# A hybrid attention layer on one core: the products with the values' weights take high and low parts at once, and VectorE's order is changed in three places

## The chip, the core and the metric

The kernel runs on one core of a Trainium2 chip. The metric is device time in microseconds. A core has five engines with queues of their own: TensorE (PE, with its weight loads as PEld), VectorE (DVE), ScalarE (ACT), GpSimd (POOL) and SyncE (SP, which here only issues DMAs). SBUF is the working memory of 128 partitions, PSUM the memory into which TensorE writes. In the profile's rows a name like L510 is line 510 of the kernel before.

## What is computed

One layer: an adaptive layer norm whose scale and shift come from a conditioning vector, a combined input projection, two groups of eight attention heads (forgetting attention with a softmax, and stick-breaking attention), SiLU gates, an output projection and a residual layer norm. Sequence 1024, width 1024, head width 64, all in float32.

```python
mod = jax.nn.silu(c) @ w_ada[layer] + b_ada[layer]       # shift, scale, gate
u = _layer_norm(x) * (1.0 + scale[:, None, :]) + shift[:, None, :]
h = u @ w_in[layer]
...
# forgetting heads, block of 128 queries
s = einsum(q, k) * scale + (f_q[..., :, None] - f_k[..., None, :])
p = softmax(where(causal, s, -inf));  out = einsum(p, v)
...
# stick-breaking heads
w = where(strict, exp(log_beta + later), 0.0);  out = einsum(w, v)
...
y = concatenate([y_fox, y_sb]) @ w_out[layer]
x = _layer_norm(alpha * x + gate[:, None, :] * y, ln_g, ln_b)
```

## The kernel before

**Two parts for each number.** Every operand of a large product is held as a rounded high part (float32r) and the remainder, the low part. A product is then high times high, low times high and high times low, added in PSUM. The high parts are made by ScalarE or GpSimd, the remainders by VectorE or GpSimd.

**The start (lines 141 to 718).** x, the conditioning weights (`wss`, one tile of 2 x 1024 columns for each of eight blocks of the width, in three buffers) and the first weights come by SP's queue in a fixed order. `mod_part` (L228) is one VectorE pass over 1024 columns that gives one block's scale or shift, so two passes a block. `u_turn` (L240) transposes x on TensorE into the PSUM tile `xT_early`; `u_round` (L246, L247) makes u's high part and the full u on ScalarE, in that same tile; `u_rest` (L259) makes the remainder on VectorE, after which the tile is free for the next block's transposes. In the loop over `kb` TensorE runs eight products of block kb's high part, transposes block kb+1, and then runs the products with the remainder. `in_turn` chains VectorE's passes in the order in which the code calls them: for kb above 1 both modulation passes of block kb+2 first, and then the remainder of block kb+1.

**The attention (lines 425 to 545 and 1031 to 1063).** Eight pairs of heads, p = 0 to 3 stick-breaking and 4 to 7 forgetting; a unit is (pair, head, block i of 128 queries), 128 in all. In iteration k of the main loop TensorE runs the scores of unit k into the one tile S (`att_scores`, L455, L456), a piece of other work from `fillers` (projections of later pairs, marked m and v), then the value products that are ready (`att_pv`, L522), then the transposes of unit k-2 (`att_transpose`, L507), and fillers again. The transposes go by groups of up to four key blocks into one of two tiles T; ScalarE copies the group's high part (L509) and VectorE subtracts for the low part (L510), into two tiles of `pt`, one for the high and one for the low parts. These remainders are the list `lows`. A unit with i of 4 or more has two groups.

**The value product.** When both units of a block j of 256 queries are transposed, `att_pv` multiplies the 2j+2 key blocks with the values, first all high parts and then all low parts, into 256 columns of PSUM. The weights are the 128 columns [v high, v low] of a head, so half of the partitions hold the product with v's high part and the others that with its low part; ScalarE copies one half (L529), VectorE adds it to the other (L530), GpSimd multiplies by the gate (L531).

**Scores.** For a forgetting head VectorE adds the forget terms to S and takes the maximum in one pass (L462), and ScalarE's exponential, a reciprocal and GpSimd's scaling follow. For a stick-breaking head ScalarE makes two sigmoids of S (L476, L478), VectorE a scan (L483, L487), GpSimd a product (L489).

**What sets the order.** TensorE's order is that of the code throughout, SP's too up to the end of the start. On the other engines a scheduler orders the work by a timeline that it models, and `after(...)` holds an instruction behind given ones. `HELD` names the iterations in which halves of the first pair's q and k, kept in SBUF as `st_held`, are written out (L269 for q, L282 for k).

Of the kernel before, what the change touches and what calls it, by code (L numbers as in the profile page):

```python
# [13 lines left out]
P = 128  # L14
# [13 lines left out]
def tile_hybrid_layer(  # L28
# [29 lines left out]

    def pt_tile(which, name, dt=F32R, shape=None):
        return big("pth" if which == 0 else "ptl", 3, name, dt, shape)  # L60

# [12 lines left out]
    RING = 5  # L74
    WARM = (4, 1, 1, 1, 0)
    NORM_ON = {6: nc.vector, 7: nc.vector}
# [65 lines left out]
    c_sb = cp.tile([P, NB], F32, tag="c_sb", name="c_sb")  # L142
    xt, wss_sb = [], []
# [299 lines left out]
    def att_scores(u, following):  # L443
# [14 lines left out]
        if p >= 4:  # L458
            a = att_tile(f"a_{p}_{h}_{i}")
            nm = sb.tile([P, 1], F32, tag="nm", bufs=4, name=f"nm_{p}_{h}_{i}")  # L460
            l = sb.tile([P, 1], F32, tag="l", bufs=4, name=f"l_{p}_{h}_{i}")
            nc.vector.tensor_tensor_reduce(out=v3(a), in0=S[:, :ns, :w], in1=v3(f),  # L462
                                           op0=ALU.add, op1=ALU.min, scale=-1.0, scalar=BIG,
                                           accum_out=nm)
            if following:
# [27 lines left out]

    def att_transpose(u):
        p, h, i = u
        a = st_w.pop(u)
        j, qo = i // 2, (i % 2) * P
        for g in range((i // 4) + 1):
            n = min(4, i + 1 - 4 * g)
            if (p, h, j, g) not in st_pt:  # L500
                st_pt[p, h, j, g] = [pt_tile(x, f"pt{x}_{p}_{h}_{j}_{g}", F32R, [P, 4, 256])
                                     for x in range(2)]
            hi, lo = st_pt[p, h, j, g]
            tp = t_tile(f"T_{p}_{h}_{i}_{g}")
            for b in range(n):
                kb = 4 * g + b
                nc.tensor.transpose(tp[:, b * P:(b + 1) * P], a[:, kb * P:(kb + 1) * P], ident)  # L507
            t3 = tp[:, :n * P].rearrange("p (a b) -> p a b", a=n)
            nc.scalar.copy(hi[:, :n, qo:qo + P], t3)  # L509
            lows[:] = [nc.vector.tensor_tensor(lo[:, :n, qo:qo + P], t3, hi.bitcast(F32)[:, :n, qo:qo + P],  # L510
                                               op=ALU.subtract)]

    y_last = []

    def att_pv(p, h, j):
        acc = pv_tile(f"pv_{p}_{h}_{j}")
        last = 2 * j + 1
        for part in range(2):
            for kb in range(last + 1):
                pt = st_pt[p, h, j, kb // 4][part]  # L520
                q0 = P if kb == last else 0
                nc.tensor.matmul(acc[:, q0:256], vt[p][:, kb, h * P:(h + 1) * P], pt[:, kb % 4, q0:],  # L522
                                 start=(part == 0 and kb == 0), stop=(part == 1 and kb == last))
        r = slice(h * HD, h * HD + HD)
# [4 lines left out]
        nc.scalar.copy(tm[r, :], acc[o, :256])  # L529
        nc.vector.tensor_tensor(yt[r, :], acc[r, :256], tm[r, :], op=ALU.add)  # L530
        nc.gpsimd.tensor_tensor(yt[r, :], yt[r, :], sgt[p][r, qs], op=ALU.mult)  # L531
        if p == NPAIR - 1:
# [25 lines left out]
    acc0 = [t_tile("st_q0"), acc_tile("st_k0"), acc_tile("st_g0"), pv_tile("st_q1"), pv_tile("st_k1", 1)]  # L558
    raw_w, split, split_at, used = {}, {}, {}, [0]
    raws = []  # L560
# [20 lines left out]
    def start_split(key):  # L581
        if key[0] == "h" or key[1] < 3:
            hi, lo = ring_w("st" + key[0] + str(key[1]))
        else:
            home = (pt_tile(1, f"hw_{key[1]}") if key[1] < 6 else pt_tile(0, "hw_6") if key[1] == 6
                    else big("sg", 2, "hw_7", F32R))
            hi, lo = home[:, :512], home[:, 512:]
# [76 lines left out]
    for kb in range(NB):  # L664
# [365 lines left out]
    for k in range(len(units) + LAG + 1):  # L1030
        if k < len(units):
# [100 lines left out]
```

## Time and profile before

| | us |
|---|---|
| median of 3 runs (690.34 to 690.57) | 690.4 |
| the profiled execution, its time | 690.46 |
| the profiled execution, its span | 688.7 |

The span runs from the first to the last instruction; 1.8 us of the execution's time lie around it. Besides the rows shown with the prediction, these groups matter. A row names line, engine, operation, what it writes and reads, its shape and count; then busy time in us and the mean of one in ns; then the idle time of the engine just before such instructions, and what ended most of it.

```profile
L509 ACT CAST pt<-T 128x512 fp32r<-128x512 f32 (+2 forms) x192 | 85.7, 480 | 17.7 <-PE T L507 13.8
...
L522 PE MATMUL pv<-pt,v 128*128 128x256 f32 (+1 forms) x640 | 82.3, 275 | 0.1
...
L462 DVE CUSTOM_DVE_ANT_0 a<-S,fb 128x1024 f32<-128x1024 f32 (+3 forms) x64 | 48.4, 756 | 21.0 <-PE S L456 10.2 <-issue 4.7 <-POOL raw_o L124 1.9
...
L228 DVE CUSTOM_DVE_ANT_0 wss<-sc_all,wss,bss_sb 128x1024 f32<-128x1024 f32 x16 | 20.0, 1282 | 7.0 <-DMA wss<-in_w_ss_dram 7.0
```

Matmuls overlap: the mean of one contains the time in which the next has begun, so 640 x 275 ns is more than the 82.3 us of busy time. The time that a product takes from its neighbours is the distance between starts.

### The profile page before, as it was taken

How to read it: one execution, taken by the hardware profiler on the slowest of the kernel's cores; microseconds unless marked ns; L12 is line 12 of the kernel's file. 1: busy time of each engine (PE TensorE's matmuls, PEld its weight loads, DVE VectorE, ACT ScalarE, POOL GpSimd, SP SyncE). 2: the span in 40 equal slices, each digit the busy share in tenths (PEclk: the TensorE clock that was granted, in tenths of full speed). 3: DMA queues.
4: the chain of work that ended last, by engine and by line, in shares of the span. 5: the costliest groups of instructions: out<-in, count | busy, mean ns of one | idle time of the engine just before them, and what ended most of it. 6: DMA issues, size and time to landing. Idle time of an engine off the chain costs nothing.

```text
span 688.7 us, 11771 instructions
## 1 busy us (share of the span) xinstructions
PE 675.7 (98%) x4031; PEld 590.9 (86%) x4031; DVE 462.8 (67%) x933; ACT 381.7 (55%) x857; POOL 405.3 (59%) x528
## 2 busy tenths in 40 slices
PE   8899999999999999999999999999999999999995
PEld 4688898888998888889988888899988889888885
DVE  6696769867668677676675665765566667774645
ACT  5566377756568666576665564655565667521000
POOL 5650179746448565556378778787794364655411
PEclk9999999999999999999999999999999999999998
DMA  8955423102102122122124454263451298143301
GB/s 339 411 206 174 154 74 78 40 24 55 39 10 72 38 54 55 39 54 54 58 82 144 144 165 156 86 192 131 126 166 58 80 292 340 58 167 113 119 31 61
DMA packets 44700, 81.59 MB, mean 118 GB/s; under 512 B 5153, under 2 KB 19297, under 8 KB 43873
## 3 DMA queue, kind: packets, MB, share of 16 engines
q1 hardware_dynamic: 43056, 76.54, 33.9%
q10 hardware_dynamic: 1584, 4.31, 2.1%
q8 instruction: 32, 0.52, 0.3%
q14 instruction: 28, 0.22, 0.1%
HBM read 60.34 MB, written 16.29 MB: 111 GB/s over the span
## 4 chain that ended last, share of the span: by engine, by line
PE 92%; DMA 4%; DVE 3%; ACT 1%; issue 0%; SPq 0%; DVEq 0%; ACTq 0%
PE pv L522 10%; PE m L294 10%; PE m L295 10%; PE m L296 10%; PE T L507 9%; PE S L456 5%; PE S L455 5%; PE o L893 4%; PE o L895 4%; PE o L894 4%; PE v L350 4%; PE v L352 4%; PE v L351 4%; DMA wss<-in_w_ss_dram 3%; PE st_late L604 1%; DMA x<-in_x_dram 1%
## 5 line engine op out<-in xcount | busy, mean ns | idle before, releaser
L294 PE MATMUL m<-uh,whi 128*128 128x512 f32 x304 | 126.3, 415 | 0.0
L295 PE MATMUL m<-ul,whi 128*128 128x512 f32 x304 | 119.7, 394 | 0.0
L296 PE MATMUL m<-uh,wlo 128*128 128x512 f32 x304 | 119.6, 393 | 0.0
L510 DVE TENSOR_TENSOR pt<-T,pt 128x512 fp32r<-128x512 f32 (+2 forms) x192 | 100.7, 551 | 18.3 <-ACT pt L509 17.1
L489 POOL TENSOR_TENSOR be<-be,kp 128x127 f32<-128x127 f32 (+3 forms) x64 | 78.5, 1227 | 37.0 <-DVE kp L487 25.8
L509 ACT CAST pt<-T 128x512 fp32r<-128x512 f32 (+2 forms) x192 | 85.7, 480 | 17.7 <-PE T L507 13.8
L483 DVE TENSOR_TENSOR_SCAN kp<-kp,floor 128x512 f32<-128x512 f32 (+2 forms) x64 | 65.1, 1018 | 32.6 <-ACT kp L476 31.7
L522 PEld LDWEIGHTS pv<-pt,v 128*128 128x128 f32 x640 | 83.0, 188 | 4.0 <-DVE pt L510 0.2
L522 PE MATMUL pv<-pt,v 128*128 128x256 f32 (+1 forms) x640 | 82.3, 275 | 0.1
L470 POOL TENSOR_SCALAR a<-a,l 128x1024 f32<-128x1024 f32 (+3 forms) x64 | 48.4, 757 | 49.6 <-DVE l L468 33.6
L296 PEld LDWEIGHTS m<-uh,wlo 128*128 128x128 f32 x304 | 57.1, 188 | 13.6
L467 ACT ACTIVATE a<-a,nm 128x1024 f32<-128x1024 f32 (+3 forms) x64 | 49.8, 778 | 33.7 <-DVE nm L462 32.9
L455 PE MATMUL S<-k,q 128*128 128x512 f32 (+5 forms) x192 | 66.4, 347 | 0.2 <-DVE nm L462 0.2
L456 PE MATMUL S<-kl,qz 128*128 128x512 f32 (+5 forms) x192 | 65.3, 341 | 0.0
L294 PEld LDWEIGHTS m<-uh,whi 128*128 128x128 f32 x304 | 57.3, 189 | 8.7 <-DVE kl L282 0.4
L295 PEld LDWEIGHTS m<-ul,whi 128*128 128x128 f32 x304 | 57.4, 189 | 7.9
L462 DVE CUSTOM_DVE_ANT_0 a<-S,fb 128x1024 f32<-128x1024 f32 (+3 forms) x64 | 48.4, 756 | 21.0 <-PE S L456 10.2
L531 POOL TENSOR_TENSOR ty<-ty,sg 64x256 f32<-64x256 f32 x64 | 47.1, 736 | 24.8 <-DVE ty L530 11.9
L476 ACT ACTIVATE kp<-S 128x128 f32<-128x128 f32 (+3 forms) x64 | 41.8, 653 | 33.4 <-PE S L456 29.9
L429 ACT CAST qz<-q 64x128 fp32r<-64x128 f32 x128 | 37.2, 295 | 34.5 <-PE S L456 33.2
L350 PE MATMUL v<-whi_v,uh 128*128 128x256 f32 (+1 forms) x192 | 56.1, 292 | 0.0
L352 PE MATMUL v<-wlo_v,uh 128*128 128x256 f32 (+1 forms) x192 | 54.1, 282 | 0.0
(289 smaller groups left out, 1589.3 us busy)
## 6 DMA issues: line engine op xcount, KB each, us to landing
raw<-in_w_qkg_dram SPq DMA_DIRECT2D x38, 256.0 KB, 2.7
wss<-in_w_ss_dram SPq DMA_DIRECT2D x6, 1024.0 KB, 9.6
x<-in_x_dram SPq DMA_DIRECT2D x8, 512.0 KB, 6.9
k<-k SPq DMA_DIRECT2D x32, 128.0 KB, 2.3
wg<-in_w_gate_dram SPq DMA_DIRECT2D x8, 512.0 KB, 4.7
raw_o<-in_w_out_dram SPq DMA_DIRECT2D x16, 256.0 KB, 3.1
fb<-f_dr ACTq DMA_DIRECT2D x8, 512.0 KB, 4.0
wo_dr<-whi_o SPq DMA_DIRECT2D x16, 256.0 KB, 2.1
```

The source lines that it names most:

```text
L294: nc.tensor.matmul(acc, hi[:, c], u_hi[kt][:, s], start=(kt == 0), stop=False)
L295: nc.tensor.matmul(acc, hi[:, c], u_lo[kt][:, s], start=False, stop=False)
L296: nc.tensor.matmul(acc, lo[:, c], u_hi[kt][:, s], start=False, stop=(kt == NB - 1))
L350: nc.tensor.matmul(acc[:, :n], u_hi[kt][:, ts_], hi[:, s], start=(kt == 0), stop=False)
L352: nc.tensor.matmul(acc[:, :n], u_hi[kt][:, ts_], lo[:, s], start=False, stop=(kt == NB - 1))
L455: nc.tensor.matmul(S[:, s, :w], qst[p][h][:, qs], kst[p][h][:, ks], start=True, stop=False)
L456: nc.tensor.matmul(S[:, s, :w], z, klo[p][:, ks], start=False, stop=True)
L483: last_dve = nc.vector.tensor_tensor_scan(rv, rv, floor[:, :ke - lo], initial=0.0, op0=ALU.mult, op1=ALU.max)
L489: nc.gpsimd.tensor_tensor(be[:, :ke - 1], be[:, :ke - 1], kp[:, 1:ke], op=ALU.mult)
L509: nc.scalar.copy(hi[:, :n, qo:qo + P], t3)
L510: lows[:] = [nc.vector.tensor_tensor(lo[:, :n, qo:qo + P], t3, hi.bitcast(F32)[:, :n, qo:qo + P], op=ALU.subtract)]
L522: nc.tensor.matmul(acc[:, q0:256], vt[p][:, kb, h * P:(h + 1) * P], pt[:, kb % 4, q0:], start=(part == 0 and kb == 0), stop=(part == 1 and ...
```

## The change

High and low parts of the attention weights come into one tile of `pt`, [128, 2, 4, 256], and one product multiplies both: 512 columns, high parts to the left, low parts to the right (the last key block 2 x 128). So 320 products take the place of 640, PSUM holds the two sums apart, and VectorE makes a second addition. The products move behind the first group of transposes of their iteration. The other users of these buffers (late tiles of x, the split weights of blocks 3 to 6) now share a double tile two by two.

VectorE's order: the maximum pass of a forgetting head waits for the last remainders; the held halves stand behind the scores and the remainders of their iteration; in the start the remainder of u stands between the two modulation passes. Also, the loads of `wss` go in two halves up to block 5, the first scalar product goes from VectorE to GpSimd, and one of the products that only keep TensorE busy in the start is left out.

```diff
-    def pt_tile(which, name, dt=F32R, shape=None):
-        return big("pth" if which == 0 else "ptl", 3, name, dt, shape)
+    def pt_tile(name, dt=F32R, shape=None):
+        return big("pt", 3, name, dt, shape or [P, 2, 1024])
...
-    WARM = (4, 1, 1, 1, 0)
+    WARM = (4, 1, 1, 0, 0)
...
     def load_x(t):
-        xi = att_tile(f"x_{t}") if t < 6 else pt_tile(0, f"x_{t}", F32)
+        if t == 6:
+            late_x.append(pt_tile("x_67", F32))
+        xi = att_tile(f"x_{t}") if t < 6 else late_x[0][:, t - 6, :]
...
-        for a in ((0, 1), (1, 2)) if kb < 2 else ((0, 2),):
+        for a in ((0, 1), (1, 2)) if kb < 6 else ((0, 2),):
...
-    nc.vector.tensor_tensor(sc, cm, c_sb, op=ALU.mult)
+    nc.gpsimd.tensor_tensor(sc, cm, c_sb, op=ALU.mult)
...
-            nc.vector.tensor_tensor_reduce(out=v3(a), in0=S[:, :ns, :w], in1=v3(f),
...
+            with after(*lows):
+                nc.vector.tensor_tensor_reduce(out=v3(a), in0=S[:, :ns, :w], in1=v3(f),
...
-    def att_transpose(u):
+    def att_transpose(u, between=()):
...
-                st_pt[p, h, j, g] = [pt_tile(x, f"pt{x}_{p}_{h}_{j}_{g}", F32R, [P, 4, 256])
-                                     for x in range(2)]
-            hi, lo = st_pt[p, h, j, g]
+                st_pt[p, h, j, g] = pt_tile(f"pt_{p}_{h}_{j}_{g}", F32R, [P, 2, 4, 256])
+            hi, lo = (st_pt[p, h, j, g][:, x] for x in range(2))
...
+            while between:
+                att_pv(*between.pop(0))
...
-        for part in range(2):
-            for kb in range(last + 1):
-                pt = st_pt[p, h, j, kb // 4][part]
-                q0 = P if kb == last else 0
-                nc.tensor.matmul(acc[:, q0:256], vt[p][:, kb, h * P:(h + 1) * P], pt[:, kb % 4, q0:],
-                                 start=(part == 0 and kb == 0), stop=(part == 1 and kb == last))
+        acc2 = acc.rearrange("p (a b) -> p a b", a=2)
+        for kb in range(last + 1):
+            pt = st_pt[p, h, j, kb // 4][:, :, kb % 4]
+            q0 = P if kb == last else 0
+            nc.tensor.matmul(acc2[:, :, q0:], vt[p][:, kb, h * P:(h + 1) * P], pt[:, :, q0:],
+                             start=(kb == 0), stop=(kb == last))
...
         nc.vector.tensor_tensor(yt[r, :], acc[r, :256], tm[r, :], op=ALU.add)
+        nc.vector.tensor_tensor(yt[r, :], acc[r, 256:], yt[r, :], op=ALU.add)
...
-            for i in parts[:1 if kb == 1 else 2]:
-                mod_terms(kb + 2, (i,))
+            mod_terms(kb + 2, parts[:1])
             rest = in_turn(u_rest, kb + 1)
-            if kb == 1:
-                mod_terms(3, (1,))
+            mod_terms(kb + 2, parts[1:])
...
-            if k in HELD:
-                m, h = HELD[k]
-                with after(*issued):
-                    evac_m(0, m, 1, held[:, m * 512:(m + 1) * 512], (h,))
...
-        while ready:
-            att_pv(*ready.pop(0))
         if LAG <= k < len(units) + LAG:
             u = units[k - LAG]
-            att_transpose(u)
+            att_transpose(u, ready)
+            if k in HELD:
+                m, h = HELD[k]
+                with after(*issued, *lows):
+                    evac_m(0, m, 1, held[:, m * 512:(m + 1) * 512], (h,))
...
+        while k >= len(units) + LAG and ready:
+            att_pv(*ready.pop(0))
```

Where it moves instructions, three places show. The first is VectorE in the start, blocks 4 and 5: `ISA wss` is a modulation pass, `ISA modc` its read-out, `ul` the remainder of u from `xT_early`. Before:

```order
L228 ISA wss_244,modc<-sc_all,wss_244,bss_sb 128x1024
L228 ISA modc 128x1
L228 ISA wss_244,modc<-sc_all,wss_244,bss_sb 128x1024
L228 ISA modc 128x1
L259 TENSOR_TENSOR ul_135<-xT_early,uh_127 128x512
L228 ISA wss_291,modc<-sc_all,wss_291,bss_sb 128x1024
```

And after the change:

```order
L230 ISA wss_245,modc<-sc_all,wss_245,bss_sb 128x1024
L230 ISA modc 128x1
L261 TENSOR_TENSOR ul_135<-xT_early,uh_127 128x512
L230 ISA wss_245,modc<-sc_all,wss_245,bss_sb 128x1024
L230 ISA modc 128x1
L230 ISA wss_293,modc<-sc_all,wss_293,bss_sb 128x1024
```

The remainder of block 3 moved ahead of the second pass of block 4; the passes themselves are as many.

The second place is VectorE in the first pair of heads, where the held half of q is written out. `pt` is a remainder, `T` its transposes, `ty` the addition after the value product, `kp` a scan. Before:

```order
L487 SCALAR_TENSOR_TENSOR kp_0_6_1297<-kp_0_6_1297,floor 128x384
L269 SCALAR_TENSOR_TENSOR q_1_249<-st_held,q_1_249 64x512
L530 TENSOR_TENSOR ty_1_1_1323<-pv_1_1_1314,ty_1_1_1323 64x256
L510 TENSOR_TENSOR pt_0_0_2_0_1329<-T_0_4_0_1330,pt_0_0_2_0_1328 128x4x128
L510 TENSOR_TENSOR pt_0_0_2_1_1338<-T_0_4_1_1339,pt_0_0_2_1_1337 128x128
L483 SCALAR_TENSOR_TENSOR kp_0_7_1354<-kp_0_7_1354,floor 128x512
```

And after the change:

```order
L490 SCALAR_TENSOR_TENSOR kp_0_6_1288<-kp_0_6_1288,floor 128x384
L512 TENSOR_TENSOR pt_0_2_0_1303<-T_0_4_0_1304,pt_0_2_0_1303 128x4x128
L534 TENSOR_TENSOR ty_1_1_1316<-pv_1_1_1311,ty_1_1_1316 64x256
L512 TENSOR_TENSOR pt_0_2_1_1322<-T_0_4_1_1323,pt_0_2_1_1322 128x128
L271 SCALAR_TENSOR_TENSOR q_1_251<-st_held,q_1_251 64x512
L535 TENSOR_TENSOR ty_1_1_1316<-pv_1_1_1311,ty_1_1_1316 64x256
L486 SCALAR_TENSOR_TENSOR kp_0_7_1340<-kp_0_7_1340,floor 128x512
```

Both remainders moved ahead of the held half, the first addition came between them, and the second addition is new.

The third place is TensorE at a value product of block j = 3 (`pv`), with the transposes `T` of the next unit around it. Before:

```order
L296 MATMUL m_2_1_1397<-uh_131,wlo_2_1_1260 128x512
L522 MATMUL pv_0_3_1501<-pt_0_0_3_0_1422,v_520 128x256 x4
L522 MATMUL pv_0_3_1501<-pt_0_0_3_1_1431,v_520 128x256 x3
L522 MATMUL pv_0_3_1501<-pt_0_0_3_1_1431,v_520 128x128
L522 MATMUL pv_0_3_1501<-pt_0_0_3_0_1423,v_520 128x256 x4
L522 MATMUL pv_0_3_1501<-pt_0_0_3_1_1432,v_520 128x256 x3
L522 MATMUL pv_0_3_1501<-pt_0_0_3_1_1432,v_520 128x128
L507 MATMUL T_1_4_0_1525<-ident,be_1_4_1389 128x128 x4
L507 MATMUL T_1_4_1_1534<-ident,be_1_4_1389 128x128
```

And after the change:

```order
L298 MATMUL m_2_1_1383<-uh_131,wlo_2_1_1251 128x512
L509 MATMUL T_1_4_0_1481<-ident,be_1_4_1375 128x128 x4
L526 MATMUL pv_0_3_1488<-pt_0_3_0_1390,v_520 128x512 x4
L526 MATMUL pv_0_3_1488<-pt_0_3_1_1411,v_520 128x512 x3
L526 MATMUL pv_0_3_1488<-pt_0_3_1_1411,v_520 128x2x128
L509 MATMUL T_1_4_1_1504<-ident,be_1_4_1375 128x128
```

Eight products stand where sixteen stood, and the first group of transposes has moved ahead of them.

More of the change, by code (lines that the diff above doesn't have):

```diff
@@ L142, in tile_hybrid_layer @@
     c_sb = cp.tile([P, NB], F32, tag="c_sb", name="c_sb")
-    xt, wss_sb = [], []
+    xt, wss_sb, late_x = [], [], []
     def load_x(t):
-        xi = att_tile(f"x_{t}") if t < 6 else pt_tile(0, f"x_{t}", F32)
+        if t == 6:
+            late_x.append(pt_tile("x_67", F32))
+        xi = att_tile(f"x_{t}") if t < 6 else late_x[0][:, t - 6, :]
         nc.sync.dma_start(xi, x[t * P:(t + 1) * P, :])
@@ L461, in att_scores @@
             l = sb.tile([P, 1], F32, tag="l", bufs=4, name=f"l_{p}_{h}_{i}")
-            nc.vector.tensor_tensor_reduce(out=v3(a), in0=S[:, :ns, :w], in1=v3(f),
-                                           op0=ALU.add, op1=ALU.min, scale=-1.0, scalar=BIG,
-                                           accum_out=nm)
+            with after(*lows):
+                nc.vector.tensor_tensor_reduce(out=v3(a), in0=S[:, :ns, :w], in1=v3(f),
+                                               op0=ALU.add, op1=ALU.min, scale=-1.0, scalar=BIG,
+                                               accum_out=nm)
             if following:
@@ L558, in tile_hybrid_layer @@
     acc0 = [t_tile("st_q0"), acc_tile("st_k0"), acc_tile("st_g0"), pv_tile("st_q1"), pv_tile("st_k1", 1)]
-    raw_w, split, split_at, used = {}, {}, {}, [0]
+    raw_w, split, split_at, used, early_w = {}, {}, {}, [0], []
     raws = []
@@ L584, in start_split @@
         else:
-            home = (pt_tile(1, f"hw_{key[1]}") if key[1] < 6 else pt_tile(0, "hw_6") if key[1] == 6
-                    else big("sg", 2, "hw_7", F32R))
+            if key[1] == 3:
+                early_w.append(pt_tile("hw_34"))
+            elif key[1] == 5:
+                early_w.append(pt_tile("hw_56"))
+            home = (early_w[-1][:, (key[1] - 3) % 2, :] if key[1] < 7 else big("sg", 2, "hw_7", F32R))
             hi, lo = home[:, :512], home[:, 512:]
```

## The prediction

> **What bounds the kernel now.** I read the page first: busy shares, the slices, the chain that ended last.
>
> ```profile
> span 688.7 us, 11771 instructions
> ...
> PE 675.7 (98%) x4031; PEld 590.9 (86%) x4031; DVE 462.8 (67%) x933; ACT 381.7 (55%) x857; POOL 405.3 (59%) x528
> ...
> PE   8899999999999999999999999999999999999995
> ...
> PE 92%; DMA 4%; DVE 3%; ACT 1%; issue 0%; SPq 0%; DVEq 0%; ACTq 0%
> PE pv L522 10%; PE m L294 10%; PE m L295 10%; PE m L296 10%; PE T L507 9%; PE S L456 5%; PE S L455 5%; PE o L893 4%; PE o L895 4%; PE o L894 4%; PE v L350 4%; PE v L352 4%; PE v L351 4%; DMA wss<-in_w_ss_dram 3%; PE st_late L604 1%; DMA x<-in_x_dram 1%
> ```
>
> TensorE is 98% busy and carries 92% of the chain; only its first two slices fall below 9 before the tail. So a stage is worth what TensorE itself spends or waits in it. A busy TensorE is not TensorE at its peak, so I read in the timeline how far apart its products start.
>
> ```profile
> 42.54 0.39 PE L604 MATMUL st_k<-uh,wlo_sth 128*128 128x512 f32 x1
> ...
> 47.44 0.28 PE L350 MATMUL st_late<-v_home,uh 128*128 128x256 f32 x1
> ...
> 53.02 0.28 PE L352 MATMUL v<-v_w,uh 128*128 128x256 f32 x1
> ```
>
> From 42.54 to 47.44 stand 21 products of 512 columns: 0.2333 us from start to start. From 47.44 to 53.02 are 47 steps of 256 columns: 0.1187 us each. Two halves cost 0.2374, a whole one 0.2333: joining two products saves 4 ns, nearly nothing. The gain of the merge has to be looked for in the groups as they run.
>
> **The merged value product.** Before, a group for one head and query block j runs 2j+2 products of the high parts and as many of the low, the last of each with 128 columns. There are 16 heads and four lengths, 4, 8, 12 and 16. The chain in order of time gives three of them to the next instruction's start, the timeline the shortest.
>
> ```profile
> 406.78 1.82 PE pv L522 x16
> ...
> 415.97 1.35 PE pv L522 x12
> ...
> 424.79 0.89 PE pv L522 x8
> ```
>
> ```profile
> 109.46 0.57 PE L522 MATMUL pv<-pt,v 128*128 128x256 f32 x4
> 109.87 0.51 PE L507 MATMUL T<-ident,be 128*128 128x128 f32 x3
> ```
>
> So 1.82, 1.35, 0.89 and 0.41. Sixteen products are 14 of 256 and two of 128 columns; 14 x 0.1187 is 1.66, so the two short ones cost 0.08 each and not half of 0.1187: after a short product the next starts late. After the change a group is 7, 5, 3 or 1 products of 512 columns and one of 2x128, priced like 256: 7 x 0.2333 + 0.1187 = 1.75, then 1.29, 0.82, 0.35. Saved: 0.07 + 0.06 + 0.07 + 0.06 = 0.26 per head, times 16 = **4.2 us**. The low bound is the pair alone, 320 x 4 ns = 1.3 us. The moving operand now has two runs of 256 a row; no row here shows such a product of this type, so a lower bound is no gain at all, and I take the middle of the groups' rows since the number of columns has set every gap so far.
>
> The Trainium skill, page "TensorE: Matmul & The Clock Gate", section "Back-to-back issue gap", puts the gap at N/2.4 + 2.5 ns, so joining two would save 2.5 ns. By it the sum of the merge would be 320 x 2.5 ns = 0.8 us, an estimate; the trace's gaps are longer at both widths (233 and 119 ns against 216 and 109), and the measured groups decide.
>
> The products now stand behind the first group of transposes; 32 of the 64 groups then have a second group of transposes behind them, so 32 more changes from transposing to products.
>
> ```profile
> 399.74 1.05 PE L507 MATMUL T<-ident,a 128*128 128x128 f32 x8
> ...
> 400.86 0.39 PE L295 MATMUL m<-ul,whi 128*128 128x512 f32 x1
> ...
> 408.44 0.83 PE L507 MATMUL T<-ident,a 128*128 128x128 f32 x6
> ...
> 409.35 0.39 PE L295 MATMUL m<-ul,whi 128*128 128x512 f32 x1
> ```
>
> Each stretch holds its transposes and one product: 1.12 for eight, 0.91 for six, so 0.105 a transpose, and 1.12 - 0.84 - 0.23 = 0.05 for the change. Bounds 0 and 32 x 0.05 = 1.6; the times are rounded to 0.01, so I take **0.5 us** lost.
>
> **The start.** One modulation sum (L228), the remainder of u (L259), the second sum: that is VectorE's new order; before, both sums stood first.
>
> ```profile
> 26.91 1.28 DVE L228 CUSTOM_DVE_ANT_0 wss<-sc_all,wss,bss_sb 128x1024 f32<-128x1024 f32 x1
> ...
> 28.12 0.68 DVE L259 TENSOR_TENSOR ul<-xT_early,uh 128x512 fp32r<-128x512 f32 x1
> ...
> 34.70 1.29 DVE L228 CUSTOM_DVE_ANT_0 wss<-sc_all,wss,bss_sb 128x1024 f32<-128x1024 f32 x1 [0.80 <-DMA wss<-in_w_ss_dram]
> ```
>
> ```profile
> 28.86 0.66 PE L240 MATMUL xT_early<-ident,x 128*128 128x128 f32 x4 [0.83 <-DVE ul L259]
> ...
> 33.95 0.66 PE L240 MATMUL xT_early<-ident,x 128*128 128x128 f32 x4 [0.94 <-DVE ul L259]
> ...
> 40.01 0.39 PE L604 MATMUL st_q<-uh,hw 128*128 128x512 f32 x1
> ```
>
> ```profile
> 14.40:47.40 33.00, 31.21 (x144) 24.53 (x145) 25.25 (x45) 20.52 (x32) 21.72 (x23) 1.00 0.89 354
> ```
>
> TensorE's transposes wait 0.83 and 0.94 for the remainder, which frees their tile. One sum (1.21 to the next start, 28.12 - 26.91) out of the way covers both: 1.8 us. But the DMA engines are 0.89 busy, so weights won't land sooner for a faster TensorE, and the halved loads reach only to block 5. Rounding u is ScalarE's:
>
> ```profile
> 38.58 0.78 ACT L246 ACTIVATE uh<-xT_early,modc 128x512 fp32r<-128x512 f32 x1 [0.23 <-PE xT_early L240]
> ```
>
> For block 6 the weights are there at 34.70. Then: first sum to 35.9, remainder of block 5 (0.7) to 36.6, second sum to 37.8, rounding (0.8) to 38.6; before, block 6 began at 40.01. So **1.3 us** stay of 1.8. Below that the bound is 0, if the two sums split by the remainder come as late as before; above it 1.8. The scalar product that goes to GpSimd and the one warming product less I count at nothing: x's loads and ScalarE's normalisation stand ahead of the first real product. The shared tiles of weights and late x keep the same bytes, three of double size for six.
>
> **The held half.** In the first pair of heads the second half of q stands ahead of the remainders.
>
> ```profile
> 117.20 1.44 DVE L269 SCALAR_TENSOR_TENSOR q<-st_held,q 64x512 fp32r<-64x512 f32 x1
> 118.67 0.43 DVE L530 TENSOR_TENSOR ty<-pv,ty 64x256 f32<-64x256 f32 x1
> 119.13 0.89 DVE L510 TENSOR_TENSOR pt<-T,pt 128x512 fp32r<-128x512 f32 x2
> ```
>
> ```profile
> 118.62 0.40 PE L456 MATMUL S<-kl,qz 128*128 128x512 f32 x1
> 119.97 0.85 PE L507 MATMUL T<-ident,be 128*128 128x128 f32 x6 [0.95 <-DVE pt L510]
> ```
>
> TensorE starts its transposes 1.35 after a product of 0.23: 1.1 us lost, since the remainders free its tiles. With q behind them they come 1.44 sooner. I count **1.1 us** won, bounds 0 and 1.1.
>
> **The second addition.** VectorE adds the low half from PSUM, 64 times, like the first addition.
>
> ```profile
> L510 DVE TENSOR_TENSOR pt<-T,pt 128x512 fp32r<-128x512 f32 (+2 forms) x192 | 100.7, 551 | 18.3 <-ACT pt L509 17.1
> ...
> L530 DVE TENSOR_TENSOR ty<-pv,ty 64x256 f32<-64x256 f32 x64 | 26.9, 420 | 37.2 <-ACT ty L529 30.7 <-POOL be L489 4.4 <-POOL be L490 0.6
> ```
>
> ```profile
> 104.00:124.00 20.00, 19.05 (x117) 16.73 (x116) 18.33 (x29) 16.09 (x34) 18.04 (x22) 1.00 0.28 70
> ...
> 364.00:540.00 176.00, 175.74 (x1089) 156.42 (x1089) 109.38 (x289) 99.99 (x249) 132.13 (x150) 1.00 0.42 133
> 540.00:612.00 72.00, 71.95 (x425) 62.82 (x424) 51.11 (x134) 42.82 (x106) 38.68 (x52) 1.00 0.58 200
> ```
>
> The third column of busy times is VectorE (after TensorE's two). 64 x 0.42 = 27 us. From 364 to 540 it is 62% busy, from 540 to 612 71%; a value group comes every 9 us there (406.78, 415.97, 424.79), that is every second unit, so 0.42 more is 5%. Nothing queued behind it (remainders, maxima, then the value tile's release two units later) is due within 0.42. I cost it at 0 there, with 27 us without that cover. From 104 to 124 VectorE is 92% busy and has no cover: three or four additions, 1.3 to 1.7 us, can show, and take back the held half's gain and more. The maxima behind the remainders cost nothing where a unit lasts four microseconds; without the cover it would be one remainder each (0.55 in the mean).
>
> **Sum** against the profiled execution, 690.46 us with its 688.7 span: -4.2 + 0.5 - 1.3 - 1.1 = -6.1, so 684.4; the median shown is 690.4, the same to 0.06. I forecast **684.4 us**.
>
> **Rivals.**
> 1. The merge saves only the pair's 4 ns, the loss at short products staying elsewhere: for it speaks the bare cadence, against it the groups' rows. Gain 1.3 in place of 4.2: 687.3.
> 2. The crowded first pair takes back start and held half: VectorE at 92%, with a TensorE that arrives 1.3 us sooner and 1.7 us more to do. Gain 4.2 - 0.5 = 3.7: 686.7. Against it: remainders now go ahead of q.
> 3. Slower: in the forgetting pairs VectorE's queue holds the next scores back. The scores have one tile; its maximum now waits for remainders, which wait behind an addition that waits for ScalarE's copy. If each of 32 pairs of units loses 0.42 to TensorE, 13.4 - 6.1 = +7.3: 697.7. It decides from 6.1/32 = 0.19 us per pair. For it: L530 already sits 30.7 us idle on the copy. Against: 38% of VectorE is free there.
> 4. With one warming product less TensorE's clock falls back before 14.4 us. The weight loads show what that costs:
>
> ```profile
> 1.55 5.82 PE L174 MATMUL sc_all<-ident 128*128 128x512 f32 x8 [1.55 <-POOL ident masks.py:199]
> ...
> 5.13 0.34 PEld L174 LDWEIGHTS sc_all<-ident 128*128 128x128 f32 x1 [0.52 <-issue]
> ...
> 5.92 0.19 PEld L174 LDWEIGHTS sc_all<-ident 128*128 128x128 f32 x1 [0.46 <-issue]
> ```
>
> 0.34 falls to 0.19 after 4.4 us of work (from 1.55, the first product). Another such 4 us at half speed would lose 2: 686.4. The Trainium skill, page "TensorE: Matmul & The Clock Gate", section "Part 1: The HAM clock gate", says that the clock halves after a window of about 3.4 us idle; transposes stand in this gap, and the rows bear out only the warming up.
>
> **How the numbers follow.** Forecast 0.62, rival 1 0.12, rival 2 0.13, rival 3 0.09, rival 4 0.04. The forecast's own range is 682.5 (start 1.8, no loss at the changes, and a few small waits of the forgetting pairs) to 686. The range 681.8 to 688.5 takes in rivals 1, 2 and 4. A measurement here tells 0.2%, 1.4 us, from no change. Faster 0.86; same 0.05, rivals 1 and 2 together (gain 0.8); slower 0.09.
>
> **What would show it.** Right: value groups of 8 products at 1.75 us; no wait of the start's transposes on the remainder at blocks 4 and 5, and block 6 at 38.7; no wait of transposes for remainders near 118; TensorE over 98% busy. Wrong: groups at 1.82 or more; scores that wait for maxima; TensorE's slices below 9 between 364 and 612; weight loads of 0.34 after 14.

## The result: 689.54 us, 0.85 us faster; 684.4 was forecast

| | before | after |
|---|---|---|
| median of 22 runs each, us | 690.39 (690.25 to 690.63) | 689.54 (689.02 to 690.19) |
| ratio of the runs, 95% interval | | 0.9988 (0.9981 to 0.9994) |
| the profiled execution, its time / span | 690.46 / 688.7 | 689.13 / 687.2 |

The change is faster by 0.12%, with an interval that ends below 1. That is less than the 0.2% that the prediction called tellable, so in its terms the outcome is "same", to which it gave 0.05; 689.54 lies above its range (681.8 to 688.5). The profiled execution of the change is one of its quicker ones, 0.4 below its median: terms read from its trace below add up to 1.6, not 0.85.

The page after the change, in the lines that answer to those of before (span, busy time by engine, the chain that ended last by engine):

```profile
span 687.2 us, 11196 instructions
...
PE 671.8 (98%) x3709; PEld 571.2 (83%) x3709; DVE 488.3 (71%) x996; ACT 381.3 (55%) x857; POOL 403.2 (59%) x529
...
PE   8999999999999999999999999999999999999995
...
PE 83%; DVE 6%; DMA 4%; ACT 3%; POOL 2%; issue 2%; DVEq 0%; POOLq 0%; ACTq 0%
```

TensorE's work fell by 3.9 us (675.7 to 671.8), the span by 1.5 only, and TensorE's part of the chain from 92% to 83%: more of it runs through VectorE, ScalarE and GpSimd, which end waits that the list of before did not have. The digits of the slices hide this; a tenth of a slice is 1.7 us. The value groups themselves, in the chain in order of time (start, us until the next piece, what):

```profile
399.30 0.35 PE pv L526 x2
...
406.57 1.75 PE pv L526 x8
...
415.68 1.28 PE pv L526 x6
...
424.21 0.81 PE pv L526 x4
```

Forecast were 0.35, 1.75, 1.29 and 0.82: the groups on TensorE are as long as forecast, to 0.01. What took it back stands in the list of TensorE's waits after the change (who waited for whom: us in total, times, longest):

```profile
PE T L509 <- DVE pt L512: 1.7, 3, 1.4
...
PE st_q L612 <- ACT uh L255: 0.9, 1, 0.9
PE st_late L352 <- DVE v L361: 0.7, 1, 0.7
PE m L296 <- DVE kl L284: 0.7, 1, 0.7
PE xT_early L242 <- DVE ul L261: 0.5, 1, 0.5
PE T L509 <- POOL be L492: 0.4, 1, 0.4
...
PE pv L526 <- DVE pt L512: 0.3, 1, 0.3
PE v L354 <- POOL wlo_v L127: 0.3, 1, 0.3
```

Before, the same list had 1.8 for `xT_early` and 0.9 for `T` behind remainders, and none of st_late, m, pv and v.

To see where each microsecond went I read from the timelines when TensorE starts the scores of each of the 128 units, and subtracted the start before the change. Negative is earlier:

| start, us, against before | before, at | after | e1 | e2 | e5 | e7 | e12 |
|---|---|---|---|---|---|---|---|
| first product of the start | 14.41 | -0.95 | -0.89 | -0.31 | -0.67 | -0.80 | -0.88 |
| first product of the values' projection | 47.44 | -1.13 | -0.87 | +0.30 | -1.20 | -1.15 | -0.95 |
| unit 0, first pair of heads | 82.60 | -0.42 | -0.12 | +0.33 | -0.50 | -1.25 | -1.08 |
| unit 16, second pair | 139.49 | +0.23 | -0.28 | +0.85 | -0.88 | -1.44 | -1.65 |
| unit 64, first forgetting pair | 349.06 | -0.28 | -0.76 | +0.39 | -0.91 | -1.92 | -3.37 |
| unit 96, seventh pair | 492.69 | -0.64 | -1.86 | +1.07 | -0.91 | -3.01 | -4.47 |
| unit 127 | 615.10 | -1.36 | -2.57 | +0.60 | -1.03 | -3.73 | -5.45 |
| end of the span | 688.74 | -1.58 | -2.77 | +0.48 | -1.04 | -3.95 | -5.67 |

(e1 to e12 are the experiments below. One trace of each was read. The start varies from trace to trace: the change and the eight experiments that share its start, e1, e3 to e6 and e8 to e10, reach unit 0 between -0.05 and -0.50.) From unit to unit, all steps under 0.15 us together are -3.9 after the change: mostly 0.07 to 0.12 at a value group, the merge. Against it stand single steps: +0.40 at unit 7, +1.54 at unit 13 (behind -1.01 at unit 12), +0.33, +0.55 and +0.26 at units 25, 33 and 41, +0.46 at unit 89, +0.62 at unit 112, and 0.7 of the start's 1.13 lost before unit 0. Four more steps, at units 85, 102, 115 and 116, are -0.2 together.

### The profile page after: what moved, and what is told of

Read it like the earlier page. It is cut to its first block, busy times and chain, and to the rows that moved or that the text cites. A ratio compares the mean times of both kernels' runs of the same rounds, so it can differ in the third digit from the quotient of the medians.

```text
span 687.2 us, 11196 instructions
## 1 busy us (share of the span) xinstructions
PE 671.8 (98%) x3709; PEld 571.2 (83%) x3709; DVE 488.3 (71%) x996; ACT 381.3 (55%) x857; POOL 403.2 (59%) x529
## 4 chain that ended last, share of the span: by engine, by line
PE 83%; DVE 6%; DMA 4%; ACT 3%; POOL 2%; issue 2%; DVEq 0%; POOLq 0%; ACTq 0%
PE m L296 9%; PE pv L526 9%; PE m L298 9%; PE m L297 9%; PE T L509 9%; PE S L458 4%; PE S L457 4%; PE o L901 4%; PE o L900 4%; PE o L899 4%; PE v L354 3%; PE v L352 3%; PE v L353 3%; DMA wss<-in_w_ss_dram 3%; PE st_late L612 1%
## 5 line engine op out<-in xcount | busy, mean ns | idle before, releaser
L512 DVE TENSOR_TENSOR pt<-T,pt 128x512 fp32r<-128x512 f32 (+2 forms) x192 | 103.1, 551 | 26.0 <-ACT pt L511 24.2
L511 ACT CAST pt<-T 128x512 fp32r<-128x512 f32 (+2 forms) x192 | 88.6, 478 | 42.0 <-PE T L509 39.1
L492 POOL TENSOR_TENSOR be<-be,kp 128x127 f32<-128x127 f32 (+3 forms) x64 | 77.1, 1204 | 37.2 <-DVE kp L490 27.6
L526 PE MATMUL pv<-pt,v 128*128 128x512 f32 x320 | 82.8, 388 | 0.3 <-DVE pt L512 0.3
L526 PEld LDWEIGHTS pv<-pt,v 128*128 128x128 f32 x320 | 55.4, 189 | 9.6 <-DVE pt L512 0.6
```

Source lines behind the costliest of these rows:

```text
L492: nc.gpsimd.tensor_tensor(be[:, :ke - 1], be[:, :ke - 1], kp[:, 1:ke], op=ALU.mult)
L526: nc.tensor.matmul(acc2[:, :, q0:], vt[p][:, kb, h * P:(h + 1) * P], pt[:, :, q0:], start=(kb == 0), stop=(kb == last))
```

## The experiments

The theories have letters, as in the expectations. **A**: the products behind the transposes call the transposes too early. **B**: the second addition makes VectorE late. **C**: the forced orders on VectorE cost the time. **F**, formed after the first four runs: a merged product needs the remainders at its first instruction, a split one only in its second half. **D** is about the start alone. Before ran beside every group of four, with a median of 690.38 to 690.40.

**e1, products ahead of the transposes.**

```diff
         fill(want[2 * k + LEAD + 1])
+        while ready:
+            att_pv(*ready.pop(0))
...
-            att_transpose(u, ready)
+            att_transpose(u)
...
```

> The change with one part undone: the merged value products stand ahead of the first group of transposes again, as before the change. Theory A (the products behind the transposes call the transposes 0.35 to 1.8 us earlier, so that they wait for T's buffers and for the weights): the new waits at units 7, 12, 25, 33, 41 and 112 go, about 3 us, and the time falls from 689.5 to about 686.5. Theory B (the second addition on VectorE delays the remainders): the waits stay, 689.2 to 689.8. Theory C (the forced orders: maxima behind remainders, held halves, modulation) likewise 689.2 to 689.8.

Measured: 687.69 us (ratio 0.9961, 0.9949 to 0.9973). One order on TensorE is worth 1.85 us: theory A has its sign, and B and C, which expect at least 689.2, are out as the whole cause. But A has not its size: of the waits that it counted as 3 us, those at units 7, 25, 33 and 41 are still there, as waits of the products for remainders (steps of 0.41, 0.26, 0.47 and 0.27), and of the one at unit 112, a projection's product (`m`) that waits for `kl`, half is left (0.34).

**e2, the merge alone.** The double tiles, the merged product and the second addition stay; the start's order, the maxima, the held halves and the products' place are those of before. The main lines:

```diff
...
-            att_transpose(u, ready)
+            att_transpose(u)
...
-            with after(*lows):
-                nc.vector.tensor_tensor_reduce(out=v3(a), in0=S[:, :ns, :w], in1=v3(f),
+            nc.vector.tensor_tensor_reduce(out=v3(a), in0=S[:, :ns, :w], in1=v3(f),
...
-                with after(*issued, *lows):
+                with after(*issued):
...
-            mod_terms(kb + 2, parts[:1])
+            for i in parts[:1 if kb == 1 else 2]:
+                mod_terms(kb + 2, (i,))
             rest = in_turn(u_rest, kb + 1)
...
```

> The kernel before with the merged product, its double tiles and its second addition alone; the order of everything else, of the start too, is that of before. If the merge saves what the prediction says (4.2 us) and costs nothing elsewhere: 686.2. Theory A expects 686 to 687, since nothing is called earlier. Theory B (the second addition takes it back): 689 to 690. Rival 1 of the prediction (4 ns a pair): 689.1.

Measured: 690.75 us (1.0005, 0.9996 to 1.0014). The merge alone gains nothing, though its small steps give -3.6 us here too. Its waits:

```profile
PE pv L525 <- DVE pt L511: 2.0, 6, 0.5
PE xT_early L242 <- DVE ul L261: 2.0, 2, 1.1
...
PE T L508 <- DVE pt L511: 1.3, 2, 1.1
```

The first row is new: value products that wait for remainders, where no product waited before. Steps of 0.27 to 0.68 stand at units 7, 11, 25, 33, 41, 69, 77 and 85, 3.4 us in all. It is slower than A and B both expect, so I formed F.

**e3, all but the merge.** Split products, without a second addition, everything else as after:

```diff
...
-        for kb in range(last + 1):
-            pt = st_pt[p, h, j, kb // 4][:, :, kb % 4]
...
+        for part in range(2):
+            for kb in range(last + 1):
+                pt = st_pt[p, h, j, kb // 4][part]
...
```

> The change without the merge: high and low products apart and no second addition, everything else as after. Predicted terms of the orders alone (start -1.3, held half -1.1, 0.5 for switches): 688.5. Theory A: the early transposes wait as in the change, so slower than before, 691.5 to 693.5. Theory B: the gain of the orders shows, 688 to 689. Theory D (the start loses its gain at the normalisation of the last block of x and nothing else happens): 690.

Measured: 698.06 us (1.0103, 1.0087 to 1.0118; five runs from 697.4 to 698.8, one of 694.33). Its waits:

```profile
PE T L508 <- DVE pt L511: 1.7, 4, 0.9
...
PE v L352 <- POOL wlo_v L127: 1.5, 2, 0.9
PE v L350 <- POOL whi_v L126: 1.1, 1, 1.1
```

The first row holds transposes at units 13, 25, 33 and 41: behind the transposes, split products lead to waits at the same places as merged ones. The other rows are split weights of the last values. 5.3 us of the time arise there: 3.75 at unit 89, and 1.53 at unit 90, where TensorE is slow and not idle. It was busy for only 2.19 of the 4.10 us from 465.00 to 469.10, and then the granted clock stood at 0.50 in place of 1.00 until 472.50, with products of 256 columns 0.21 us apart in place of 0.12. Without these 5.3 us the time would be 692.8, as A expects. In the transfers of the trace the fetch of these weights issues at 453.81 and lands at 460.05; in the change at 450.37 and 454.21. SyncE's queue (start, us, what; a row of x2 holds the wait of its second transfer) shows what stands ahead of it in e3:

```profile
441.29 8.90 SPq L542 DMA_DIRECT2D y_dr<-ty  x2
450.33 0.49 SPq L853 DMA_DIRECT2D wo_dr<-whi_o  x1
...
453.81 0.43 SPq L122 DMA_DIRECT2D raw_v<-in_w_v_dram  x1
```

The store of a value group's result waits for the group, and the fetch waits behind the store. The fetch itself took 6.2 us here and 3.8 in the change; why was not tried, and neither was the wait of 0.7 for `kl` at unit 112.

**e4, no second addition.**

```diff
-        nc.vector.tensor_tensor(yt[r, :], acc[r, 256:], yt[r, :], op=ALU.add)
```

> The change without its second addition: the products of the low parts of the attention weights are computed and left out of the result. Theory A: VectorE's 27 us less cost TensorE little, 688.8 to 689.5. Theory B: the remainders come 0.4 us sooner wherever an addition stood ahead of them, 686 to 687.

Measured: 689.56 us (0.9987, 0.9979 to 0.9996), the change's own time to 0.02. 24.5 us of VectorE's work (488.3 to 463.8 busy) gone and nothing gained in sum: B's 686 to 687 is out. Its trace against the change's shows two parts: 0.6 less in small steps (0.2 of it at units 12 and 13), but 0.99 more at unit 89 (1.45 in place of 0.46), where TensorE waits for the split weights of the last values. So the addition is not free everywhere; why unit 89 is worse without it was not tried.

**e5, the orders alone.** The diffs of e3 and of e1 together: neither merge nor new place.

> The kernel before with the orders of the change alone: maxima behind remainders, held halves behind remainders, the start's order, its halved loads, the scalar product on GpSimd and one warming product less; high and low products apart, ahead of the transposes, no second addition. If gains add up (the merge alone gave +0.3, merge and orders 687.7, so the orders 3 us): 687.4. Theory F (part of the orders' 3 us exists only with the merge: a merged product needs the remainders from its first instruction, a split one only from its second half, so the maxima behind remainders win time only for the merged one): start 0.4 and held half 0.7 alone, 689.0 to 689.6.

Measured: 689.56 us (0.9988, 0.9979 to 0.9997), in F's range. Between units 16 and 96 the orders are worth 0.03 us; the merge costs 0.2 there without them (e2), and both together win 1.6 (e1). From unit 64, where the maxima begin, to unit 96 e5 gains 0.00. So the maxima behind the remainders pay for the merged product alone.

**e6, maxima free again.** e1, and

```diff
-            with after(*lows):
-                nc.vector.tensor_tensor_reduce(out=v3(a), in0=S[:, :ns, :w], in1=v3(f),
+            nc.vector.tensor_tensor_reduce(out=v3(a), in0=S[:, :ns, :w], in1=v3(f),
```

> As e1 (merged products ahead of the transposes, all orders), but the maxima of the forgetting heads need not wait for the remainders. Theory F: the waits of the value products for remainders at units 69, 77 and 85 that the merge alone showed come back, 1.7 us, so 689.4. If the maxima's order has no price: 687.7.

Measured: 689.80 us (0.9993, 0.9984 to 1.0002): this one wait on VectorE is worth 2.1 us to the merged product. The timeline shows how. e6, VectorE and then TensorE:

```profile
440.27 0.69 DVE L464 CUSTOM_DVE_ANT_0 a<-S,fb 128x512 f32<-128x512 f32 x1
...
440.88 1.15 DVE L511 TENSOR_TENSOR pt<-T,pt 128x512 fp32r<-128x512 f32 x2
```

```profile
440.72 0.40 PE L298 MATMUL m<-uh,wlo 128*128 128x512 f32 x1
441.63 2.01 PE L525 MATMUL pv<-pt,v 128*128 128x512 f32 x8 [0.51 <-DVE pt L511]
```

And e1, where the remainders go first:

```profile
439.47 1.16 DVE L512 TENSOR_TENSOR pt<-T,pt 128x512 fp32r<-128x512 f32 x2
440.54 0.68 DVE L465 CUSTOM_DVE_ANT_0 a<-S,fb 128x512 f32<-128x512 f32 x1
```

```profile
439.92 0.40 PE L298 MATMUL m<-uh,wlo 128*128 128x512 f32 x1
440.21 2.01 PE L526 MATMUL pv<-pt,v 128*128 128x512 f32 x8
```

In e1 the group begins 0.29 after the last projection product, in e6 0.91: the maximum of 0.69 stands ahead of its remainders. That is 0.62 lost, and a split group's eight high products, 0.9 us, would have covered it: before the change, with the maxima as free, no product waits.

**e7, the last block of x behind the values' remainder.** e1, with the normalisation of block 7 of x moved on VectorE.

```diff
-                for t in (6, 7):
-                    norm_stats(t)
-                    norm_x(t)
+                for t in (6, 7):
+                    norm_stats(t)
+                norm_x(6)
...
     v_first(0, late_acc[:, 0, :])
+    with after(*v_done):
+        norm_x(7)
```

> As e1, but the normalisation of the last block of x stands on VectorE behind the remainders of the first value tile in place of ahead of the second. Theory D (the start's gain of 0.9 is lost there, in a wait of 0.77 before 53.19): the wait goes and the gain stays, 686.9. Rival: something else holds TensorE back at the same place or a little later (the next tile's remainder, the transposes of the last block of x), 687.4 to 687.9.

Measured: 686.77 us (0.9948, 0.9935 to 0.9960), D's number. The timeline after the change, TensorE and VectorE, where the start's gain was lost:

```profile
52.90 0.39 PE L352 MATMUL st_late<-v_home,uh 128*128 128x256 f32 x1 [0.73 <-DVE v L361]
```

```profile
51.11 0.29 DVE L361 TENSOR_TENSOR v<-st_late,v 128x128 fp32r<-128x128 f32 x1
51.83 0.81 DVE L217 TENSOR_SCALAR x<-x,mv_a,rs_a 128x1024 f32<-128x1024 f32 x1 [0.43 <-POOL rs_a L192]
52.55 0.29 DVE L361 TENSOR_TENSOR v<-st_late,v 128x128 fp32r<-128x128 f32 x1
```

VectorE stood idle for 0.43 and then normalised for 0.8, with the remainder that TensorE waited for behind it. In e7 the same remainder starts at 51.73, and TensorE's next product at 52.08.

**e8, other work ahead.** e1, with one more piece of other work ahead of the products in six iterations.

```diff
-        fill(want[2 * k + LEAD + 1])
+        fill(want[2 * k + LEAD + 1] + (k in (6, 10, 12, 24, 32, 40)))
```

> As e1, but in the six iterations in which a merged product waits for its remainder (0.49, 0.28, 0.24, 0.24, 0.45, 0.25, 1.95 in all) one piece of the other work that stood behind the products and transposes goes ahead of them, 1.4 us. Theory F: the remainder is there in time and up to 1.95 us go, 685.8 to 686.6. Rival (late products and transposes make the next step late instead, ScalarE's copies and the scores behind them): 687.3 to 688.5.

Measured: 687.68 us (0.9961, 0.9948 to 0.9973): nothing gained. The products' waits went, and transposes wait instead, above all those of the next unit, now 1.4 us nearer (steps of 0.91, 0.70 and 0.82 at units 14, 34 and 42):

```profile
PE T L509 <- DVE pt L512: 1.9, 3, 0.7
```

At units 14 and 42 they wait for the remainder that frees T's tile: it is the next unit's, not the one that the products had waited for.

**e9 and e10, where the products' place costs.** The change, with the products ahead of the transposes in the first pair (k < 16), or in the sixth (80 to 95), alone.

```diff
         fill(want[2 * k + LEAD + 1])
+        while ready and k < 16:
+            att_pv(*ready.pop(0))
```

> The change, but in the first pair of heads alone the products stand ahead of the transposes again. Theory A, by place: between units 11 and 16 the profile of the change loses 0.8 us against that of e1 (transposes at 124.42 that come 1.35 too early for a remainder), so 689.5 - 0.8 = 688.7, and the wait at unit 13 falls to e1's 0.3. If the products behind the transposes cost evenly over the 64 groups (1.85 us / 64 each, 8 of them here): 689.3.

> The change, but in the sixth pair of heads alone the products stand ahead of the transposes again. Theory A, by place: later products put the stores of their results later into SyncE's queue, and the fetch of the value weights behind these; the wait for GpSimd's split of them at unit 89 (0.46 in the change, 1.45 in e4) goes: 688.5 to 689.0. Spread evenly (8 groups of 64): 689.3.

Measured: 688.15 us (0.9968, 0.9955 to 0.9980) and 688.73 us (0.9978, 0.9969 to 0.9987): 1.4 and 0.8 of the 1.85 that e1 gains. A holds by place; together they are 2.2, more than e1's gain, by less than the width of any of the three intervals (1.2 us and more). In e10 the step at unit 89 is gone, with the fetch at 448.67 where the change had 450.37. The first pair after the change, VectorE and then TensorE:

```profile
118.75 1.91 DVE L271 SCALAR_TENSOR_TENSOR q<-st_held,q 64x512 fp32r<-64x512 f32 x1
120.69 0.43 DVE L535 TENSOR_TENSOR ty<-pv,ty 64x256 f32<-64x256 f32 x1
121.15 1.22 DVE L486 TENSOR_TENSOR_SCAN kp<-kp,floor 128x512 f32<-128x512 f32 x1
122.41 1.28 DVE L490 TENSOR_TENSOR_SCAN kp<-kp,floor 128x512 f32<-128x512 f32 x1
123.60 1.00 DVE L512 TENSOR_TENSOR pt<-T,pt 128x512 fp32r<-128x512 f32 x2
```

```profile
122.67 0.39 PE L298 MATMUL m<-uh,wlo 128*128 128x512 f32 x1
124.42 0.63 PE L509 MATMUL T<-ident,be 128*128 128x128 f32 x4 [1.35 <-DVE pt L512]
```

In e9 the same stretch of VectorE reads:

```profile
119.20 0.69 DVE L271 SCALAR_TENSOR_TENSOR q<-st_held,q 64x512 fp32r<-64x512 f32 x1
120.33 1.22 DVE L486 TENSOR_TENSOR_SCAN kp<-kp,floor 128x512 f32<-128x512 f32 x1 [0.44 <-ACT kp L479]
121.58 1.28 DVE L490 TENSOR_TENSOR_SCAN kp<-kp,floor 128x512 f32<-128x512 f32 x1
122.78 1.00 DVE L512 TENSOR_TENSOR pt<-T,pt 128x512 fp32r<-128x512 f32 x2
```

Two things meet. The remainders come 0.8 later after the change, since the held half takes 1.91 in place of 0.69 (last section) and the second addition stands behind it. And transposes, which need T's tiles back from these remainders, stand directly behind the projections' products at 122.67, where in e9 a value group comes first, at 123.50.

**e11 and e12, both distances kept.** e7, with one piece of other work ahead in the iterations 6, 7, 10 to 17, 24, 25, 32, 33, 40 and 41 (e11); or e7, in e8's six iterations with the piece ahead of the transposes and the products behind them (e12):

```diff
...
+        fill(want[2 * k + LEAD + 1] + (k in (6, 10, 12, 24, 32, 40)))
+        while ready and k not in (6, 10, 12, 24, 32, 40):
+            att_pv(*ready.pop(0))
...
             att_transpose(u)
+            while ready:
+                att_pv(*ready.pop(0))
...
```

> As e7 (merged products ahead of the transposes, x7's normalisation behind the first value tile's remainder), with one piece of other work ahead of the products, not in six iterations alone, as in e8, but also in those that follow (7, 11, 13 to 17, 25, 33, 41), so that the next transposes aren't called 1.4 us sooner. If e8 lost its gain to these (0.6 to 0.9 at four places): 685.0 to 685.8. If the wait only moves on by one unit more: 686.8.

> As e7, but in the six iterations in which a merged product waits for its remainder one piece of other work goes ahead of the transposes, and the products stand behind them: the transposes come 0.4 us later than in e7 (1.4 less a group of products), the products 1.4 and the transposes later. Theory F with both distances kept: most of 1.95 us goes, 685.0 to 685.8. Rival (the second wait of each place is T's buffer, as in e8): 686.5 to 687.

Measured: 685.28 us (0.9929, 0.9916 to 0.9941) and 684.87 us (0.9922, 0.9908 to 0.9936). e11 lies in the range of its expectation, e12 0.13 below its own. Both beat before and change, e12 by 5.5 and 4.7 us. Its page and waits:

```profile
PE 671.0 (98%) x3709; PEld 573.0 (84%) x3709; DVE 486.5 (71%) x996; ACT 380.5 (56%) x857; POOL 404.2 (59%) x529
...
PE 90%; DMA 4%; DVE 4%; ACT 1%; issue 1%; SPq 0%; DVEq 0%
```

```profile
PE T L511 <- DVE pt L514: 0.5, 2, 0.3
```

TensorE has almost the change's work, and 90% of the chain.

## Why the prediction was wrong

| term of the sum | forecast | found |
|---|---|---|
| merged products, on TensorE | -4.2 | -3.9 in the change, -4.1 in e1 and e7 |
| changes from transposes to products | +0.5 | at most 0.2 (small steps of the change and of e1) |
| start | -1.3 | -1.13 at the first product of the values' projection, -0.42 at unit 0 |
| held half | -1.1 | -1.01 at unit 12, +1.54 at unit 13 |
| second addition | 0 | 0 in sum (e4) |
| maxima behind remainders | 0 | 0 split (e5), -2.1 merged (e6) |
| products behind transposes, as a wait | none | +1.85 (e1) |
| merged product waiting for remainders, six places | none | +1.9 (e7 to e12) |

The rows come from different runs and overlap (e1's 1.85 holds most of the 1.54 at unit 13), so they are not one sum. The change's own trace up to unit 127 gives one: merge -3.9, start -0.42, held half +0.53, the steps at units 7, 25, 33, 41, 89 and 112 +2.6, the rest -0.2, in all -1.4 in place of -6.1. The largest part of the 4.7 between them are the waits of 2.6 that the sum had at nothing; the held half is 1.6, the start 0.9.

**The step that failed** is the way in which the merged product was priced: as columns on TensorE alone, "Saved: 0.07 + 0.06 + 0.07 + 0.06 = 0.26 per head". That was right to a few tenths, and rival 1, which had the gain at 1.3, was wrong. But a split group reads its remainders only when its high half is through, 0.2 to 0.9 us later, and that time was cover that the sum did not name. Merging takes it away. Where the remainder is late, the product waits (e2, e6); where the products stand behind the transposes, the transposes wait for T's tiles, which the same remainder frees (the change, units 13, 25 and 41; at unit 33 the last to end, by 0.04, was GpSimd's product that they read); where other work is moved ahead without more, the next unit's transposes wait (e8).

The second half of that step is the products' new place, which the prediction priced as "32 more changes from transposing to products" alone. These cost next to nothing: two merged products and eight transposes, from the first of them to the second product behind, take 1.46 us in both orders (five of six such places in the change and in e1; the sixth 1.35 and 1.34). The place itself is enough for the waits: with split products behind the transposes (e3) transposes wait at units 13, 25, 33 and 41, with split products ahead of them (e5) only the step of 0.47 at unit 13 is left. So at 25, 33 and 41 either edit alone, the merge or the place, brings the wait; with neither (before, e5) it is covered. The steps at units 89 and 112 wait for other things, split weights and `kl`; the first goes when the products of that pair stand ahead (e10), the second stays open.

**The start** was nearly right at its place: the first product came 0.95 sooner, which the sum counted at nothing, block 6 began at 38.83 (38.7 forecast), and of the two waits one of 0.52 was left, at 36.70. The step that failed there is "x's loads and ScalarE's normalisation stand ahead of the first real product" as the only look at x: the last two blocks of x are normalised on VectorE, behind the start's loop, and a start that is a microsecond sooner meets them. e7 shows that this alone took the gain: with it mended -1.25 reach unit 0.

**The held half** moved as forecast, and the wait near 118 went. "With q behind them they come 1.44 sooner" stopped one unit too early: the pass of q has to run at some time, and behind the remainders it ran into the next unit's. Without merge and new place (e5) the two steps are -0.83 and +0.47, a gain of 0.4 in place of 1.1; the new place made the second one larger (e9).

**Rivals.** Rival 2 named the crowded first pair and gave 686.7; the place was right, but the crowd was for the most part the held half and the early transposes: without the second addition the step at unit 13 is still 1.11 of 1.54 (e4). Rival 3, the scores held back by VectorE's queue, fell: VectorE is 67% busy from 364 to 540 now (118.70 of 176), and the one wait of scores for a maximum is 0.2, as before. The maxima's order, priced at 0, was needed (e6). Rival 4 fell too: after 13.46 each weight load of a product takes 0.19.

The forecast's 684.4 is, within half a microsecond, what e12 takes (684.87), with the three hidden waits mended. That is luck in part: in e12 the start gives 1.08, and the held half, with -0.99, +0.51 and +0.40 at units 12 to 14, next to nothing in place of 1.1; the 0.5 for switches, few of which e12 makes, comes back and covers half of that.

## What to carry to other kernels

Joining two products takes the first one's time away from the second one's operand. Before joining, look up when that operand is written, and count the first half's duration as cover that goes.

A wait for a late result is removed by making it earlier or its reader later. Swapping the order of two readers of the same result can change no more than the name of the one that waits (units 25, 33 and 41, the change against e1); moving filler ahead of one reader draws the next reader nearer (e8).

An order on another engine that costs nothing today can be what a merged instruction needs tomorrow: price such edits together, not one by one.

## What was unexpected of the hardware

The held half of q, the same pass over 64x512 in SBUF, took 0.69 us in e9, 1.44 before and 1.91 after the change. GpSimd's queue after the change shows what ran beside it:

```profile
118.34 1.77 POOL L492 TENSOR_TENSOR be<-be,kp 128x895 f32<-128x895 f32 x1
```

The pass was recorded from 118.75 to 120.66; GpSimd's product, which reads SBUF too, ended at 120.11. From there to the pass's end are 0.55, less than the 0.69 that it takes alone, so the end of the pass seems to hang on the end of GpSimd's product (GpSimd's spans are rough). The other kernels bear this out. In ten of the fourteen traces the last GpSimd instruction begun before the pass, a product or a subtraction with two inputs in SBUF, was still under way when the pass was recorded as begun, and had at least 0.23 us to go: the pass took 0.78 to 2.31 us and ended 0.54 to 0.55 us after that instruction, in all ten. In the other four (e1, e6, e7, e9) it had ended or had 0.05 us to go, and the pass took 0.69. In e9 GpSimd's product ran ahead of it (117.47 to 119.25), and the next one, behind the pass, took 1.17 in place of some 0.73. The Trainium skill, page "SBUF — State Buffer", section "Who interferes with whom", says that a VectorE instruction with two inputs in SBUF contends with a GpSimd instruction that reads SBUF, that the shared pair of ports is an exclusive lock, and that the order of issue decides who blocks. These rows agree; no run here measured the two by themselves.

TensorE's merged product, whose moving operand is two runs of 256 columns, ran at the pace of one run of 512: seven of them and a short one in the forecast 1.75 us.
